# Instance normalisation: statistics of the last tile in one pass

## The chip, the core and the metric

The kernel runs on one core of one Trainium2 chip. The metric is device time in microseconds. Executions of one program spread here by about 2 us, with now and then one that is 4 to 12 us longer, so a time is quoted as a median with its range, and the difference of two kernels comes from runs taken in turn on the same chip. All runs count as fast. Times read off a trace count from the start of the profiled span; the metric is 1.7 us longer than that span.

## The reference

```python
x = np.random.randn(8, 64, 32, 64, 64).astype(np.float32)     # 512 instances of 131072 elements
mean = np.mean(x, axis=(2, 3, 4), keepdims=True)
var = np.var(x, axis=(2, 3, 4), keepdims=True)
out = ((x - mean) / np.sqrt(var + eps)).astype(np.float32)
```

268 MB are read and 268 MB are written. Little is computed per byte.

## The kernel before

Each tile is 128 partitions x 12288 elements (6 MB), three chunks of 4096 to a partition. 42 such tiles go through four buffers; two small parts of 2 MB go first. A tile is loaded whole, worked on, and stored. An instance lies over several partitions, so its sums are put together by a matmul with a matrix of averages (`avg`) and a small mask (`belongs`). Two such hand-overs follow each other: means, then the sums of squares around them. VectorE and ScalarE share the elements.

```python
    def tile_on_vector(eng, t, lane, c1, c3, c4, c16):
        # sums of chunk 0 and of a piece of chunk 2
        for j, part in ((0, chunk[0]), (3, t[:, COLS - TURN :])):
            eng.reduce_sum(out=column(a, SUMS, j), in_=part, axis=AXIS)._wait_ge(
                landed[lane], c16).then_inc(summed[lane], 1)
        over_instance(...)                                   # mask, matmul, sum, mask, sum: means
        eng.tensor_scalar(out=chunk[0], in0=chunk[0], scalar1=column(a, MEANS, 0), ...)   # centre
        eng.tensor_tensor_reduce(out=unused[2][:], in0=chunk[0], in1=chunk[0], ...)       # squares
        over_instance(...)                                   # the same again: variances
        eng.reciprocal(...); eng.tensor_mul(...)             # scale, shift
        eng.tensor_scalar(out=chunk[0], ...).then_inc(done[lane], 1)    # x * scale
        eng.tensor_scalar(out=chunk[1], ...).then_inc(done[lane], 1)    # x * scale + shift

    def tile_on_scalar(eng, t, lane, c1, c3, c4, c16, dst, last=False):
        # ... sums of chunk 1 and most of chunk 2; later squares of chunks 1 and 2; the root ...
        at = 0
        if last:
            at = CHUNK
            eng.dma_start(out=dst[:, :at], in_=chunk[0])._wait_ge(
                done[lane], c3 - 2).then_inc(stored[lane], 16)          # a third goes out early
        eng.activation(out=chunk[2], in_=chunk[2], func=Act.Identity, ...)   # x * scale + shift
        eng.dma_start(out=dst[:, at:], in_=t[:, at:])._wait_ge(done[lane], c3).then_inc(
            stored[lane], 16)
```

(The loads are issued by SyncE, each when its buffer has been stored.)

## Time and profile before

| | kernel before |
|---|---|
| median of 3 runs (range) | 1247.86 us (1247.49 to 1249.13) |
| the profiled execution | 1249.99 us, span 1248.3 us |
| DMA rate over the span | 430 GB/s |
| last tile in its buffer, work starts | 1211.60 |
| first store of the last tile issued | 1231.17 |
| last packet of the last store ends | 1246.84 |

A load or a store is cut into packets, which 16 DMA engines move. In the packet records of these traces a full tile is 128 packets of 48 KB, eight to an engine, and one small packet closes each engine's share. The *landing* of a tile is the moment when the last engine has closed its share of the load.

The prediction below shows the page's main lines, the last chain and the windows of the tail. What the statistics cost can be read from the groups of instructions with shapes kept apart (before the bar: line, engine, operation, shapes, count; after it: busy us in all and mean ns of one; then the idle time ahead of it).

```profile
L160 DVE TENSOR_REDUCE small<-slot 128x1 f32<-128x4096 f32 x42 | 185.6, 4420 | 288.7 <-DMA slot<-in_x_dram 288.7
L174 DVE CUSTOM_DVE_ANT_0 unused<-slot 128x4096 uint8<-128x4096 f32 x42 | 185.9, 4426 | 1.4
L167 DVE TENSOR_SCALAR slot<-slot,small 128x4096 f32<-128x4096 f32 x42 | 98.8, 2353 | 1.5
```

To take VectorE's statistics of one chunk the kernel reads it three times: 4.42 us for the sum, 2.35 us to centre it, 4.43 us for the squares.

### The profile page before, as it was taken

How to read it: one execution, taken by the hardware profiler on the slowest of the kernel's cores; microseconds unless marked ns; L12 is line 12 of the kernel's file. 1: busy time of each engine (PE TensorE's matmuls, PEld its weight loads, DVE VectorE, ACT ScalarE, POOL GpSimd, SP SyncE). 2: the span in 40 equal slices, each digit the busy share in tenths (PEclk: the TensorE clock that was granted, in tenths of full speed). 3: DMA queues.
4: the chain of work that ended last, by engine and by line, in shares of the span. 5: the costliest groups of instructions: out<-in, count | busy, mean ns of one | idle time of the engine just before them, and what ended most of it. 6: DMA issues, size and time to landing. Idle time of an engine off the chain costs nothing.

```text
span 1248.3 us, 1975 instructions
## 1 busy us (share of the span) xinstructions
PE 53.5 (4%) x180; PEld 44.9 (4%) x180; DVE 817.8 (66%) x734; ACT 754.8 (60%) x437; POOL 2.7 (0%) x15
## 2 busy tenths in 40 slices
PE   1000000000000000000000000000000000000000
PEld 0000000000000000000000000000000000000000
DVE  4886666666666666666666666666666666666664
ACT  4776655555665666666555566666665665556663
POOL 0000000000000000000000000000000000000000
DMA  9999999999999999999999999999999999999997
GB/s 400 423 429 449 432 428 428 432 443 433 430 428 443 435 430 428 435 441 432 428 432 438 438 430 428 430 447 430 430 430 436 439 432 430 428 446 432 430 432 340
DMA packets 13106, 536.89 MB, mean 430 GB/s; under 512 B 1456, under 2 KB 1456, under 8 KB 1712
## 3 DMA queue, kind: packets, MB, share of 16 engines
q1 hardware_dynamic: 6624, 268.44, 49.9%
q10 hardware_dynamic: 6480, 268.44, 49.7%
q14 instruction: 2, 0.02, 0.0%
HBM read 268.44 MB, written 268.44 MB: 430 GB/s over the span
## 4 chain that ended last, share of the span: by engine, by line
DMA 77%; DVE 11%; ACT 8%; PE 1%; issue 0%; SPq 0%; ACTq 0%
DMA slot<-in_x_dram 40%; DMA out_dram<-slot 38%; ACT unused L224 7%; DVE small L160 5%; DVE slot L196 2%; DVE slot L203 2%; PE psum L260 1%; ACT unused L217 0%; DVE small L140 0%; DVE small L128 0%; DVE small L134 0%; DVE small L146 0%; ACT slot L243 0%; ACT small L231 0%; DVE small L188 0%
## 5 line engine op out<-in xcount | busy, mean ns | idle before, releaser
L160 DVE TENSOR_REDUCE small<-slot 128x1 f32<-128x4096 f32 x84 | 255.3, 3081 | 288.7 <-DMA slot<-in_x_dram 288.7
L217 ACT ACTIVATE unused<-slot 128x4096 uint8<-128x4096 f32 x84 | 249.3, 2968 | 319.8 <-DMA slot<-in_x_dram 318.6
L224 ACT ACTIVATE unused<-slot,small 128x4096 uint8<-128x4096 f32 x84 | 310.8, 3701 | 65.3 <-DVE small L146 65.3
L174 DVE CUSTOM_DVE_ANT_0 unused<-slot 128x4096 uint8<-128x4096 f32 x42 | 185.9, 4426 | 1.4
L243 ACT ACTIVATE slot<-slot,small 128x4096 f32<-128x4096 f32 x42 | 159.7, 3802 | 21.1 <-DVE small L191 18.0
L203 DVE TENSOR_SCALAR slot<-slot,small 128x4096 f32<-128x4096 f32 x42 | 101.1, 2407 | 0.0
L167 DVE TENSOR_SCALAR slot<-slot,small 128x4096 f32<-128x4096 f32 x42 | 98.8, 2353 | 1.5
L260 PE MATMUL psum<-small,avg 128*128 128x12 f32 (+1 forms) x168 | 50.3, 375 | 1153.2 <-DVE small L128 1153.2
L196 DVE TENSOR_SCALAR slot<-slot,small 128x4096 f32<-128x4096 f32 x42 | 98.6, 2346 | 0.0
L260 PEld LDWEIGHTS psum<-small,avg 128*128 128x128 f32 x168 | 42.1, 311 | 1161.4 <-DVE small L128 1161.4
L134 DVE TENSOR_REDUCE small<-psum 128x3 f32<-128x12 f32 x84 | 14.2, 169 | 58.0 <-PE psum L260 58.0
L231 ACT ACTIVATE small<-small,eps_t 128x3 f32<-128x3 f32 x42 | 12.5, 299 | 62.6 <-DVE small L146 62.6
L128 DVE TENSOR_TENSOR small<-small,belongs 128x12 f32<-128x12 f32 x84 | 14.3, 170 | 31.4 <-ACT unused L224 29.5
L188 DVE RECIPROCAL small<-small 128x3 f32<-128x3 f32 x42 | 7.4, 175 | 15.4 <-ACT small L231 15.4
L140 DVE TENSOR_TENSOR small<-small,belongs 128x9 f32<-128x9 f32 x84 | 14.3, 170 | 2.9
L217 ACT ACTIVATION_READ_ACCUMULATOR unused<-slot 128x1 f32 x84 | 15.7, 187 | 0.0
L224 ACT ACTIVATION_READ_ACCUMULATOR unused<-slot,small 128x1 f32 x84 | 15.7, 187 | 0.0
L146 DVE TENSOR_REDUCE small<-small 128x3 f32<-128x9 f32 x84 | 13.6, 162 | 2.9
L280 DVE TENSOR_REDUCE small<-slot 128x1 f32<-128x1200 f32 (+1 forms) x4 | 4.7, 1208 | 7.6 <-DMA slot<-in_x_dram 7.6
L320 ACT ACTIVATE unused<-slot 128x1360 uint8<-128x1360 f32 (+1 forms) x4 | 4.2, 1059 | 5.8 <-DMA slot<-in_x_dram 5.3
L191 DVE TENSOR_TENSOR small<-small 128x3 f32<-128x3 f32 x42 | 6.8, 161 | 1.4
L326 ACT ACTIVATE unused<-slot,small 128x2608 uint8<-128x2608 f32 x2 | 4.9, 2469 | 1.9 <-DVE small L283 1.9
(32 smaller groups left out, 29.4 us busy)
## 6 DMA issues: line engine op xcount, KB each, us to landing
slot<-in_x_dram SPq DMA_DIRECT2D x42, 6144.0 KB, 47.1
out_dram<-slot ACTq DMA_DIRECT2D x41, 6144.0 KB, 47.1
out_dram<-slot ACTq DMA_DIRECT2D x3, 2048.0 KB, 23.7
out_dram<-slot ACTq DMA_DIRECT2D x1, 4096.0 KB, 11.8
slot<-in_x_dram SPq DMA_DIRECT2D x2, 1280.0 KB, 8.1
slot<-in_x_dram SPq DMA_DIRECT2D x2, 768.0 KB, 9.5
```

What stands on the lines that cost most here:

```text
L128: eng.tensor_tensor(out=block(a, by_both, n, m), in0=spread(a, at, m), in1=belongs[:, :, :m], op=Alu.mult,)._wait_ge(*wait).then_inc(steps ...
L134: eng.tensor_reduce(out=a[:, by_instance : by_instance + n], in_=p.rearrange("p (n m) -> p n m", m=m), axis=AXIS, op=Alu.add,)._wait_ge(st ...
L140: eng.tensor_tensor(out=block(a, by_chunk, n, n), in0=spread(a, by_instance, n), in1=belongs[:, :, :n].rearrange("p i c -> p c i"), op=Alu ...
L160: eng.reduce_sum(out=column(a, SUMS, j), in_=part, axis=AXIS)._wait_ge(landed[lane], c16).then_inc(summed[lane], 1)
L167: eng.tensor_scalar(out=chunk[0], in0=chunk[0], scalar1=column(a, MEANS, 0), scalar2=None, op0=Alu.add,)._wait_ge(centred[lane], c1).then_ ...
L174: eng.tensor_tensor_reduce(out=unused[2][:], in0=chunk[0], in1=chunk[0], scale=1.0, scalar=0.0, op0=Alu.mult, op1=Alu.add, accum_out=colum ...
L196: eng.tensor_scalar(out=chunk[0], in0=chunk[0], scalar1=column(a, SCALES, 0), scalar2=None, op0=Alu.mult,)._wait_ge(scaled[lane], c1).then ...
L203: eng.tensor_scalar(out=chunk[1], in0=chunk[1], scalar1=column(a, SCALES, 1), scalar2=column(a, SHIFTS, 1), op0=Alu.mult, op1=Alu.add,)._w ...
L217: eng.activation(out=unused[j - 1][:, : part.shape[1]], in_=part, func=Act.Identity, accum_out=column(a, SUMS, j),)._wait_ge(landed[lane], ...
L224: eng.activation(out=unused[j - 1][:], in_=chunk[j], func=Act.Square, bias=column(a, MEANS, j), accum_out=column(a, SQUARES, j),)._wait_ge ...
L243: eng.activation(out=chunk[2], in_=chunk[2], func=Act.Identity, scale=column(a, SCALES, 2), bias=column(a, SHIFTS, 2),)._wait_ge(shifted[l ...
L260: eng.matmul(out=p[:, col : col + THIRDS * m], lhsT=avg[PART][:], rhs=a[:, at + m : at + m + THIRDS * m], start=True, stop=True,)._wait_ge ...
```

## The change

For the last tile alone the statistics are taken in one pass. VectorE runs `bn_stats`, which gives mean and variance together, over chunk 0 and most of chunk 1. ScalarE finds the mean of its own pieces and then their squares around this own mean, without a hand-over between. The four pieces differ in size; masks weighted by size (`weighs`) put their means and variances together. All other tiles stay as they are; the setup on GpSimd gets six more small steps.

```diff
+    GROUP = 480
+    SHARE = 7 * GROUP
+    first_of = (0, CHUNK, 2 * CHUNK, CHUNK + SHARE)
+    sizes = (CHUNK, SHARE, CHUNK, CHUNK - SHARE)
+    groups = [(i * 512, 512) for i in range(CHUNK // 512)]
+    groups += [(CHUNK + i * GROUP, GROUP) for i in range(SHARE // GROUP)]
...
+    def last_on_vector(eng, t, lane, c1, c3, c4, c16):
+        for g, (at, size) in enumerate(groups):
+            i = eng.bn_stats(out=stats[:, g, :], in_=t[:, at : at + size])
...
+        step(eng.bn_aggr(out=a[:, 0:2], in_=stats[:, :split, :]))
+        step(eng.bn_aggr(out=a[:, 2:4], in_=stats[:, split:, :]))
+        eng.wait_ge(meant, 2)
+        weigh(means, BOTH)
+        hand_out(0, INST, CHUNKED, NEGATIVE, m, True)        # matmul: means of the instances
...                                                          # how far each piece's mean is off, squared
+        eng.wait_ge(spread_, 2)
+        step(eng.tensor_add(...))                            # its variance + that square
+        weigh(a[:, TOTAL : TOTAL + m], BOTH2)
+        hand_out(n * m, INST2, CHUNKED2, FOUND, n, False)    # matmul: variances
+        eng.wait_ge(took_root, 1)
...                                                          # reciprocal, shift, both chunks scaled
+    def last_on_scalar(eng, t, lane, c1, c3, c4, c16, dst):
...                                                          # own means, own squares, root, stores
-            on_tile(eng, slots[k % SLOTS][:], k % SLOTS, c, 3 * c, 4 * c, 16 * c, *more)
+            step = on_last if k == n_tiles - 1 else on_tile
+            step(eng, slots[k % SLOTS][:], k % SLOTS, c, 3 * c, 4 * c, 16 * c, *more)
```

More of the change, by code (lines that the diff above doesn't have):

```diff
@@ L72 @@
     belongs = sbuf("belongs", [P, THIRDS, THIRDS + 1])
+    GROUP = 480
+    SHARE = 7 * GROUP
+    first_of = (0, CHUNK, 2 * CHUNK, CHUNK + SHARE)
+    sizes = (CHUNK, SHARE, CHUNK, CHUNK - SHARE)
+    PIECES = len(sizes)
+    belongs4 = sbuf("belongs4", [P, THIRDS, PIECES])
+    weighs = sbuf("weighs", [P, THIRDS, PIECES])
+    groups = [(i * 512, 512) for i in range(CHUNK // 512)]
+    groups += [(CHUNK + i * GROUP, GROUP) for i in range(SHARE // GROUP)]
+    stats = sbuf("stats", [P, len(groups), 6])
+    late = sbuf("late", [P, 96])
     small = [sbuf(f"small{i}", [P, 72]) for i in range(LANES)]
@@ L98 @@
     moved = semaphores("moved", SLOTS)
+    went, meant, leaned, spread_, multiplied, took_root = semaphores("late", 6)
     shrunk = semaphores("shrunk")
@@ L210, in tile_on_vector, with tile_on_scalar @@
         )._wait_ge(shifted[lane], c1).then_inc(done[lane], 1)
-    def tile_on_scalar(eng, t, lane, c1, c3, c4, c16, dst, last=False):
+    def tile_on_scalar(eng, t, lane, c1, c3, c4, c16, dst):
         a = small[lane]
@@ L236, in tile_on_scalar @@
         )._wait_ge(gathered[lane], c1).then_inc(rooted[lane], 1)
-        at = 0
-        if last:
-            at = CHUNK
-            eng.dma_start(out=dst[:, :at], in_=chunk[0])._wait_ge(
-                done[lane], c3 - 2
-            ).then_inc(stored[lane], 16)
         eng.activation(
@@ L249, in tile_on_scalar @@
         )._wait_ge(shifted[lane], c1).then_inc(done[lane], 1)
-        eng.dma_start(out=dst[:, at:], in_=t[:, at:])._wait_ge(done[lane], c3).then_inc(
+        eng.dma_start(out=dst, in_=t)._wait_ge(done[lane], c3).then_inc(
             stored[lane], 16
@@ L266, in tile_on_tensor, with step, weigh, hand_out @@
             )._wait_ge(before[lane], c1).then_inc(after[lane], 1)
+    BIAS, BOTH, INST, CHUNKED, NEGATIVE, FAR, FAR2, TOTAL = 8, 10, 22, 25, 37, 41, 45, 49
+    BOTH2, INST2, CHUNKED2, FOUND, ROOTED, SCALED, SHIFTED = 53, 65, 68, 77, 80, 83, 86
+    def last_on_vector(eng, t, lane, c1, c3, c4, c16):
+        a, p = late, psum[lane]
+        n, m = THIRDS, PIECES
+        means, variances = a[:, 0 : 2 * m : 2], a[:, 1 : 2 * m : 2]
+        count = 0
+        def step(i):
+            nonlocal count
+            if count:
+                i._wait_ge(went, count)
+            i.then_inc(went, 1)
+            count += 1
+        def weigh(what, to):
+            step(
+                eng.tensor_tensor(
+                    out=block(a, to, n, m),
+                    in0=what.unsqueeze(1).to_broadcast([P, n, m]),
+                    in1=weighs[:],
+                    op=Alu.mult,
+                )
+            )
+        def hand_out(col, inst, at, to, k, negate):
+            eng.tensor_reduce(
+                out=a[:, inst : inst + n],
+                in_=p[:, col : col + n * m].rearrange("p (n m) -> p n m", m=m),
+                axis=AXIS,
+                op=Alu.add,
+            )._wait_ge(multiplied, 1 if col == 0 else 2).then_inc(went, 1)
+            nonlocal count
+            count += 1
+            step(
+                eng.tensor_tensor(
+                    out=block(a, at, k, n),
+                    in0=a[:, inst : inst + n].unsqueeze(1).to_broadcast([P, k, n]),
+                    in1=belongs4[:, :, :k].rearrange("p i c -> p c i"),
+                    op=Alu.mult,
+                )
+            )
+            step(
+                eng.tensor_reduce(
+                    out=a[:, to : to + k],
+                    in_=block(a, at, k, n),
+                    axis=AXIS,
+                    op=Alu.add,
+                    negate=negate,
+                )
+            )
+        for g, (at, size) in enumerate(groups):
+            i = eng.bn_stats(out=stats[:, g, :], in_=t[:, at : at + size])
+            if g == 0:
+                i._wait_ge(landed[lane], c16)
+        i.then_inc(went, 1)
+        count += 1
+        split = CHUNK // 512
+        step(eng.bn_aggr(out=a[:, 0:2], in_=stats[:, :split, :]))
[3 more added lines that the diff above has]
+        hand_out(0, INST, CHUNKED, NEGATIVE, m, True)
+        step(
+            eng.tensor_add(
+                out=a[:, FAR : FAR + m], in0=means, in1=a[:, NEGATIVE : NEGATIVE + m]
+            )
+        )
+        far = a[:, FAR : FAR + m]
+        step(eng.tensor_mul(out=a[:, FAR2 : FAR2 + m], in0=far, in1=far))
+        eng.wait_ge(spread_, 2)
+        step(
+            eng.tensor_add(
+                out=a[:, TOTAL : TOTAL + m], in0=variances, in1=a[:, FAR2 : FAR2 + m]
+            )
+        )
+        weigh(a[:, TOTAL : TOTAL + m], BOTH2)
+        hand_out(n * m, INST2, CHUNKED2, FOUND, n, False)
+        eng.wait_ge(took_root, 1)
+        step(
+            eng.reciprocal(out=a[:, SCALED : SCALED + n], in_=a[:, ROOTED : ROOTED + n])
+        )
+        step(
+            eng.tensor_mul(
+                out=a[:, SHIFTED : SHIFTED + n],
+                in0=a[:, NEGATIVE : NEGATIVE + n],
+                in1=a[:, SCALED : SCALED + n],
+            )
+        )
+        assert count == STEPS
+        for j in (0, 1):
+            part = t[:, j * CHUNK : (j + 1) * CHUNK]
+            eng.tensor_scalar(
+                out=part,
+                in0=part,
+                scalar1=column(a, SCALED, j),
+                scalar2=column(a, SHIFTED, j),
+                op0=Alu.mult,
+                op1=Alu.add,
+            )._wait_ge(went, STEPS).then_inc(done[lane], 1)
@@ new lines @@
+    WEIGHED, WEIGHED2, VARIED, STEPS = 4, 11, 14, 16
+    def last_on_scalar(eng, t, lane, c1, c3, c4, c16, dst):
+        a = late
+        mine = [(j, t[:, first_of[j] : first_of[j] + sizes[j]]) for j in (2, 3)]
+        for j, part in mine:
+            eng.activation(
+                out=unused[j - 2][:, : sizes[j]],
+                in_=part,
+                func=Act.Identity,
+                scale=1.0 / sizes[j],
+                accum_out=column(a, 0, 2 * j),
+            )._wait_ge(landed[lane], c16).then_inc(meant, 1)
+        for j, _ in mine:
+            eng.activation(
+                out=column(a, BIAS, j - 2),
+                in_=column(a, 0, 2 * j),
+                func=Act.Identity,
+                scale=-(sizes[j] ** -0.5),
+            )._wait_ge(meant, 2).then_inc(leaned, 1)
+        for j, part in mine:
+            eng.activation(
+                out=unused[j - 2][:, : sizes[j]],
+                in_=part,
+                func=Act.Square,
+                scale=sizes[j] ** -0.5,
+                bias=column(a, BIAS, j - 2),
+                accum_out=column(a, 0, 2 * j + 1),
+            )._wait_ge(leaned, 2).then_inc(spread_, 1)
+        eng.activation(
+            out=a[:, ROOTED : ROOTED + THIRDS],
+            in_=a[:, FOUND : FOUND + THIRDS],
+            func=Act.Sqrt,
+            bias=eps_t[:, 0:1],
+        )._wait_ge(went, VARIED).then_inc(took_root, 1)
+        eng.dma_start(out=dst[:, :CHUNK], in_=t[:, :CHUNK])._wait_ge(
+            done[lane], c3 - 2
+        ).then_inc(stored[lane], 16)
+        eng.activation(
+            out=t[:, 2 * CHUNK :],
+            in_=t[:, 2 * CHUNK :],
+            func=Act.Identity,
+            scale=column(a, SCALED, 2),
+            bias=column(a, SHIFTED, 2),
+        )._wait_ge(went, STEPS).then_inc(done[lane], 1)
+        eng.dma_start(out=dst[:, CHUNK:], in_=t[:, CHUNK:])._wait_ge(
+            done[lane], c3
+        ).then_inc(stored[lane], 16)
@@ L273, with last_on_tensor @@
+    def last_on_tensor(eng, t, lane, c1, c3, c4, c16):
+        for col, at, ready_at in ((0, BOTH, WEIGHED), (12, BOTH2, WEIGHED2)):
+            eng.matmul(
+                out=psum[lane][:, col : col + THIRDS * PIECES],
+                lhsT=avg[PART][:],
+                rhs=late[:, at : at + THIRDS * PIECES],
+                start=True,
+                stop=True,
+            )._wait_ge(went, ready_at).then_inc(multiplied, 1)
     HEAD = 2560
@@ L362, with over_tiles @@
     ]
-    def over_tiles(eng, on_part, on_tile, with_target=False):
+    def over_tiles(eng, on_part, on_tile, on_last, with_target=False):
         for m, (lane, t) in enumerate(parts):
@@ L381, in over_tiles @@
             c = k // SLOTS + 1
-            more = (out_t[k], k == n_tiles - 1) if with_target else ()
-            on_tile(eng, slots[k % SLOTS][:], k % SLOTS, c, 3 * c, 4 * c, 16 * c, *more)
+            more = (out_t[k],) if with_target else ()
+            step = on_last if k == n_tiles - 1 else on_tile
+            step(eng, slots[k % SLOTS][:], k % SLOTS, c, 3 * c, 4 * c, 16 * c, *more)
     def load_all(eng):
@@ L472, in set_up @@
         )
+        for to, c in ((slice(0, THIRDS), slice(0, THIRDS)), (slice(3, 4), slice(1, 2))):
+            step(eng.tensor_copy(out=belongs4[:, :, to], in_=belongs[:, :, c]))
+        for j, size in enumerate(sizes):
+            step(
+                eng.tensor_scalar(
+                    out=weighs[:, :, j : j + 1],
+                    in0=belongs4[:, :, j : j + 1],
+                    scalar1=float(size),
+                    scalar2=None,
+                    op0=Alu.mult,
+                )
+            )
         return count
@@ L477 @@
     nc.vector.wait_ge(ready, set_by)
-    over_tiles(nc.vector, part_on_vector, tile_on_vector)
+    over_tiles(nc.vector, part_on_vector, tile_on_vector, last_on_vector)
     nc.tensor.wait_ge(ready, set_by)
-    over_tiles(nc.tensor, part_on_tensor, tile_on_tensor)
+    over_tiles(nc.tensor, part_on_tensor, tile_on_tensor, last_on_tensor)
     nc.scalar.preload_act_table(Act.Sqrt)
     nc.scalar.wait_ge(ready, set_by)
-    over_tiles(nc.scalar, part_on_scalar, tile_on_scalar, with_target=True)
+    over_tiles(nc.scalar, part_on_scalar, tile_on_scalar, last_on_scalar, with_target=True)
     wait_for_stores(nc.scalar)
```

## The prediction

> **What bounds the kernel now.** I began with the page: busy time by engine, the slices and the DMA queues. They say that the stream of transfers is the limit.
>
> ```profile
> PE 53.5 (4%) x180; PEld 44.9 (4%) x180; DVE 817.8 (66%) x734; ACT 754.8 (60%) x437; POOL 2.7 (0%) x15
> DMA  9999999999999999999999999999999999999997
> q1 hardware_dynamic: 6624, 268.44, 49.9%
> q10 hardware_dynamic: 6480, 268.44, 49.7%
> ```
>
> VectorE works for 66% of the span, ScalarE for 60%, but the DMA row reads 9 in every slice but the last, and the two queues' packets fill 99.6% of sixteen engines' time. So only what lies outside this stream can be saved: its head, and the tail in the last slice (a 7). The change touches only the last of 42 full tiles, so I read the tail: first the chain that ended last, then the same stretch by windows.
>
> ```profile
> 1211.60 6.09 DVE small L160 x2
> ...
> 1219.19 7.50 ACT unused L224 x4
> ...
> 1228.87 2.27 DVE slot L196
> 1231.15 0.02 issue
> 1231.17 0.35 ACTq L240
> 1231.52 0.05 issue
> 1231.57 3.80 ACT slot L243
> ```
>
> The columns are start, length, what. The last tile is in the buffer at 1211.60. Sums take 6.09 us, squares 7.50 us, the two hand-overs through TensorE fill the places cut out, one third is scaled, and at 1231.17, 19.57 us after the landing, the first third's store is issued. The chain makes it look as if every microsecond saved there came off the end. The windows say whether DMA has something else to do meanwhile (columns: stretch and length, busy time and count of PE, PEld, DVE, ACT, POOL, clock, DMA share, GB/s):
>
> ```profile
> 1219.20:1226.70 7.50, 0.00 (x0) 0.00 (x0) 6.78 (x3) 7.48 (x4) 0.00 (x0) 1.00 1.00 433
> 1226.70:1231.20 4.50, 0.59 (x2) 0.50 (x2) 3.33 (x8) 0.30 (x1) 0.00 (x0) 1.00 0.15 66
> 1231.20:1232.00 0.80, 0.00 (x0) 0.00 (x0) 0.80 (x1) 0.43 (x1) 0.00 (x0) 1.00 0.00 0
> 1232.00:1237.00 5.00, 0.00 (x0) 0.00 (x0) 1.46 (x1) 3.37 (x1) 0.00 (x0) 1.00 1.08 459
> 1237.00:1246.90 9.90, 0.00 (x0) 0.00 (x0) 0.00 (x0) 0.00 (x0) 0.00 (x0) 1.00 0.94 404
> ```
>
> Until 1226.70 DMA is full (share 1.00) with the store of the tile before. Then come 4.50 us at a share of 0.15. That is not idle. The DMA view of 1227 to 1231.9 has what moves there:
>
> ```profile
> DMA packets 12, 0.29 MB, mean 60 GB/s; under 512 B 6, under 2 KB 6, under 8 KB 6
> ```
>
> Twelve packets start there: six of 48 KB and six small ones, which close an engine's share. Following the packet records, eleven or so of the 16 engines end their share of the store before between 1226.48 and 1227.31, but the last five end at 1228.35, 1229.55, 1230.21, 1231.15 and **1231.54**. A 48 KB packet takes 1.81 us on the late engines as on the others, and they have no gap between packets: they are simply behind. All tiles near the end show the same lag, 4 to 6 us between the first and the last engine. The last two stores then start on all engines at 1232.02 to 1232.17, 0.85 us after the issue, take 8 packets of 0.61 us and 8 of 1.22 us on each (14.67 us), and end at 1246.84. The span ends 1.45 us later.
>
> **What the Trainium skill says.** The page "DMA: Bandwidth & Descriptors", section "Why a DMA increments its semaphore by 16 and not by 1", says that a transfer runs on up to 16 engines that finish independently, each adding one to the semaphore behind its own data. The trace agrees: sixteen small packets close each store, here spread over 5 us. "VectorE: DVE Perf Modes", section "The perf-mode tier table", has tensor_reduce in the 1x mode only; here (4420 - 1743) / (4096 - 1536) = 1.046 ns per element, about one per cycle of the page's 0.96 GHz. "ScalarE: Activation LUTs", section "What ACT_TABLE_LOAD costs", gives 0.833 ns per element for an ACTIVATE; here (3617 - 2320) / 1536 = 0.844. No page that I found states the duration of bn_stats or bn_aggr, and no instruction of this trace is one, so I estimate both.
>
> **The change, part by part.** Times count from the landing at 1211.60.
>
> VectorE loses the two reductions (6.09), the centring of a third (2.35) and its squares (4.43 and the accumulator's read). It gains 15 bn_stats over 4096 + 3360 = 7456 elements. At the reduction's 1.046 ns that is 7.80 us. For the fixed cost, the second reduction of 1536 adds 6.08 - 4.42 = 1.66 us behind the first, 0.05 more than its elements; I choose 0.10 for an instruction that puts out six numbers, so 1.5 for 15. Statistics: **9.3 us**. Two bn_aggr over 48 and 42 numbers: a small instruction steps on in 0.20 (1218.58, 1218.79, 1218.99 in the timeline); I choose 0.37 each, 0.74 in all. Then come 13 small steps (weigh, sum, spread, sum, add, square, add, weigh, sum, spread, sum, reciprocal, shift) at 0.20: 2.6. TensorE is crossed twice; the weighing at 1217.71 to the reduction at 1218.58 is 0.87, less its own 0.20, so 0.67 each, 1.34 in all. The root adds 0.33 (1227.97 to 1228.50, less 0.20). Scaling and shifting the first third takes 2.41 (the row of L203, the same form). Sum: 9.3 + 0.74 + 2.6 + 1.34 + 0.33 + 2.43 = 16.74, so the first store is issued at about **1228.3**, 2.8 us earlier.
>
> ScalarE goes beside this: sums of 4096 and 736 elements (3.62 + 0.88, with an accumulator read), two one-element biases (0.55), squares of the same pieces (3.71 + 0.87 + 0.19). It ends at 9.9. VectorE wants its means after the aggregation at 10.0, its variances near 12. ScalarE should not be waited for, but with little in hand. It scales its third after the issue, as before: 0.40 + 3.80, so the second store is issued near 1232.6, while the first still runs.
>
> GpSimd gets six more small steps ahead of the loop, some 0.27 us each by its timeline, 1.6 in all: ready at 5.9 instead of 4.23, and the first piece lands at 7.10. Free. No other tile changes.
>
> What reaches the end? On the eleven early engines the last stores could start at 1228.3 + 0.85 = 1229.2 and end at 1243.9. The last engine is still busy until 1231.55. It takes the new packets without a gap and ends at 1231.55 + 14.67 = 1246.2. A store is done when all engines are. So of 2.8 us **only about 0.6 remains**: 1246.84 - 1246.2. From the median of 1247.86 that makes about 1247.2.
>
> **Rivals.** (a) All 2.8 us come off, to 1245.0: so it would be if the late engines had little lag in the timed runs, or caught up once the others were done. For it: the chain of waits, and I know the lag from one execution. Against it: the lag is there in each of the last tiles, and packets keep their 1.81 us when only few engines work. (b) bn_stats needs two cycles per element. Then statistics take 7.8 us more, the issue falls at 1236.1, the early engines decide too, and the time is about 4.9 us over the one before, 1252.8. Nothing in the profile speaks for it, but nothing rules it out. (c) ScalarE becomes the wait: it would have to be 2 us later than worked out to matter at all, and another 2.4 us of chain would be hidden behind the late engine anyway (issue up to 1230.7 still reaches it in time). (d) Nothing measurable: the three runs before lie 1.64 us apart, more than the gain.
>
> **Range and chances.** I give the late engine 65%, (a) or a part of it 25%, (b) under 10%. Together with run-to-run differences of about a microsecond: predicted 1247.0, a little below 1247.2 for the share of (a), range 1245.0 to 1248.6. Two per cent are 25 us, more than the whole tail from landing to last issue, so within 2% is almost sure: 0.98, with 0.01 on each side.
>
> **What would show it.** In the changed profile: bn_stats near 0.6 us each, 9.3 us together; ScalarE's squares done before VectorE adds its variances; the first store issued near 1228.3 on this trace's clock, or 16.7 us behind the landing; early engines closing the last store near 1243.9 and the last ones 2 us later; an end moved by well under the 2.8 us. The prediction is wrong if bn_stats takes over 0.75 us (the issue then comes after 1230.6), if the combining steps wait on ScalarE, or if the end moves by as much as the issue, which would mean that the late engines' lag isn't what holds the last store.

## The result and the profile after

| | before | changed |
|---|---|---|
| median of 6 runs each, in turn | 1247.69 us | 1247.62 us |
| range | 1247.19 to 1249.13 | 1247.16 to 1248.97 |
| profiled execution: time, span | 1249.99, 1248.3 | 1247.61, 1245.9 |
| work on the last tile starts | 1211.60 | 1208.34 |
| first store issued (after the start of work) | 1231.17 (19.57) | 1224.72 (16.38) |
| last packet ends (after the start of work) | 1246.84 (35.24) | 1244.31 (35.97) |

The ratio of the two kernels is 0.9999, with a 95% interval of 0.9986 to 1.0012: no difference. The 2.8 us of rival (a), 0.9978, lie outside it. (It is the mean time of one kernel's fast runs over that of the other's of the same rounds, so not quite the ratio of the medians.)

Beware of the spans. They differ by 2.4 us, near to what the chain saves, and tempt one to say that the chain's gain came off the end. But the execution profiled of the kernel before was one of its slower ones (1249.99 us where the median is 1247.69), and the last tile landed 3.26 us later in it. Nothing of the change happens before that landing, apart from setup. Counted from the start of the last tile's work, the end is no earlier in the changed kernel (35.97 us against 35.24).

The chain itself did what it was built for. Groups of the changed kernel:

```profile
L335 DVE BATCH_NORM_STATS2 stats<-slot 128x6 f32<-128x512 f32 x8 | 4.8, 678 | 7.2 <-DMA slot<-in_x_dram 7.2
L335 DVE BATCH_NORM_STATS2 stats<-slot 128x6 f32<-128x480 f32 x7 | 4.0, 642 | 0.0
L341 DVE BATCH_NORM_AGGREGATE late<-stats 128x2 f32<-128x48 f32 x1 | 0.4, 371 | 0.0
L342 DVE BATCH_NORM_AGGREGATE late<-stats 128x2 f32<-128x42 f32 x1 | 0.3, 344 | 0.0
```

The 15 `bn_stats` overlap a little: alone some 0.66 us, in a row 8.77 us. From its timeline (start, length, engine, line, operation), the moments that matter:

```profile
1208.34 8.76 DVE L335 BATCH_NORM_STATS2 stats<-slot 128x6 f32<-128x512 f32 x15 [7.20 <-DMA slot<-in_x_dram]
1217.71 0.19 ACT L408 ACTIVATION_READ_ACCUMULATOR unused<-slot,late 128x1 f32 x1
1219.79 0.17 DVE L355 TENSOR_TENSOR late<-late 128x4 f32<-128x4 f32 x1
1224.72 0.35 ACTq L422 DMA_DIRECT2D out_dram<-slot  x1
```

ScalarE's squares are complete at 1217.90, and VectorE adds variances only at 1219.79: ScalarE is not waited for. The chain view of the changed kernel ends so (start, length, what):

```profile
1208.34 8.77 DVE stats L335 x15
1222.28 2.42 DVE slot L375
1225.12 3.80 ACT slot L425
```

It follows instructions and stops at ScalarE's last one, 17 us before the end of the span. What happens after, the windows of the changed kernel tell (columns as in the prediction's windows; the DMA share and GB/s are the last two):

```profile
1224.70:1226.60 1.90, 0.00 (x0) 0.00 (x0) 1.90 (x1) 1.48 (x1) 0.00 (x0) 1.00 0.96 414
1226.60:1231.40 4.80, 0.00 (x0) 0.00 (x0) 0.41 (x1) 2.32 (x1) 0.00 (x0) 1.00 0.98 420
1231.40:1241.20 9.80, 0.00 (x0) 0.00 (x0) 0.00 (x0) 0.00 (x0) 0.00 (x0) 1.00 1.00 431
1241.20:1244.40 3.20, 0.00 (x0) 0.00 (x0) 0.00 (x0) 0.00 (x0) 0.00 (x0) 1.00 0.07 31
1244.40:1245.90 1.50, 0.00 (x0) 0.00 (x0) 0.00 (x0) 0.00 (x0) 0.00 (x0) 1.00 0.00 0
```

The stretch of little traffic that lay at 1226.70 to 1231.20 before (share 0.15) is full now (0.98). It has not gone: it has moved to the very end, 3.2 us at a share of 0.07. The DMA view has what starts in the changed kernel between 1241.7 and the end, and in the kernel before between 1246.6 and the end:

```profile
DMA packets 5, 0.07 MB, mean 16 GB/s; under 512 B 3, under 2 KB 3, under 8 KB 3
```

```profile
DMA packets 16, 0.00 MB, mean 0 GB/s; under 512 B 16, under 2 KB 16, under 8 KB 16
```

Each engine closes its share of a store with one small packet. Before, all sixteen are closed within 0.17 us, since all had waited for the same issue. Changed, thirteen engines are closed by 1241.7, and two 32 KB packets and three closing ones follow. One of the sixteen engines closes 1.9 us after all others, at 1244.31. It had also been the last with the store of the tile before, by 1.9 us.

### The profile page after: what moved, and what is told of

It is laid out like the page before. It is cut to its first block, busy times and chain, and to the rows that moved or that the text cites. A ratio compares the mean times of both kernels' runs of the same rounds, so it can differ in the third digit from the quotient of the medians.

```text
span 1245.9 us, 2001 instructions
## 1 busy us (share of the span) xinstructions
PE 53.5 (4%) x180; PEld 44.9 (4%) x180; DVE 815.1 (65%) x749; ACT 750.8 (60%) x439; POOL 4.0 (0%) x21
## 4 chain that ended last, share of the span: by engine, by line
another core or an unknown queue 46%; DMA 39%; DVE 7%; ACT 5%; SPq 1%; PE 1%; issue 1%; ACTq 0%; DVEq 0%
DMA slot<-in_x_dram 20%; DMA out_dram<-slot 19%; ACT unused L239 4%; DVE small L176 2%; DVE slot L219 1%; DVE slot L212 1%; DVE stats L335 1%; SPq L580 1%; PE psum L269 1%; ACT unused L232 0%; ACT slot L425 0%; DVE slot L375 0%; DVE small L156 0%; DVE small L144 0%
## 5 line engine op out<-in xcount | busy, mean ns | idle before, releaser
L176 DVE TENSOR_REDUCE small<-slot 128x1 f32<-128x4096 f32 x82 | 249.2, 3081 | 278.2 <-DMA slot<-in_x_dram 278.2
L232 ACT ACTIVATE unused<-slot 128x4096 uint8<-128x4096 f32 x82 | 243.3, 2968 | 308.6 <-DMA slot<-in_x_dram 307.4
L239 ACT ACTIVATE unused<-slot,small 128x4096 uint8<-128x4096 f32 x82 | 303.4, 3700 | 63.7 <-DVE small L162 63.7
L190 DVE CUSTOM_DVE_ANT_0 unused<-slot 128x4096 uint8<-128x4096 f32 x41 | 181.4, 4425 | 1.4
L252 ACT ACTIVATE slot<-slot,small 128x4096 f32<-128x4096 f32 x41 | 155.9, 3801 | 18.0 <-DVE small L207 18.0
L219 DVE TENSOR_SCALAR slot<-slot,small 128x4096 f32<-128x4096 f32 x41 | 98.7, 2407 | 0.0
L183 DVE TENSOR_SCALAR slot<-slot,small 128x4096 f32<-128x4096 f32 x41 | 96.5, 2353 | 1.5
L269 PE MATMUL psum<-small,avg 128*128 128x9 f32 (+1 forms) x164 | 49.1, 375 | 1122.0 <-DVE small L144 1122.0
L212 DVE TENSOR_SCALAR slot<-slot,small 128x4096 f32<-128x4096 f32 x41 | 96.2, 2346 | 0.0
L335 DVE BATCH_NORM_STATS2 stats<-slot 128x6 f32<-128x512 f32 (+1 forms) x15 | 8.8, 661 | 7.2 <-DMA slot<-in_x_dram 7.2
L393 ACT ACTIVATE unused<-slot 128x4096 uint8<-128x4096 f32 (+1 forms) x2 | 4.4, 2209 | 8.0 <-DMA slot<-in_x_dram 8.0
```

Of the source, the lines that this page charges most:

```text
L219: eng.tensor_scalar(out=chunk[1], in0=chunk[1], scalar1=column(a, SCALES, 1), scalar2=column(a, SHIFTS, 1), op0=Alu.mult, op1=Alu.add,)._w ...
L232: eng.activation(out=unused[j - 1][:, : part.shape[1]], in_=part, func=Act.Identity, accum_out=column(a, SUMS, j),)._wait_ge(landed[lane], ...
L239: eng.activation(out=unused[j - 1][:], in_=chunk[j], func=Act.Square, bias=column(a, MEANS, j), accum_out=column(a, SQUARES, j),)._wait_ge ...
L269: eng.matmul(out=p[:, col : col + THIRDS * m], lhsT=avg[PART][:], rhs=a[:, at + m : at + m + THIRDS * m], start=True, stop=True,)._wait_ge ...
L335: i = eng.bn_stats(out=stats[:, g, :], in_=t[:, at : at + size])
```

## The experiments

The theory (L): DMA is busy from start to end, each engine works off its own share, and the engine furthest behind sets the end. An earlier issue helps that engine only if it would otherwise run dry. The rival (C): the chain of the last tile sets the end, and each microsecond taken from it or added to it shows. In a trace the two can be told by three moments, taken from the packet records: the landing of the last tile, for which the work waits; the moment when the late engine is *free*, that is, done with the store of the tile before; and the end. 16 packets of the last stores take an engine 14.55 us without a pause. So *end - free - 14.55* is the hole in the late engine's work, what the chain can add to the end. (Where all engines start the last stores together, the 16 packets take 14.67 us. So 0.12 us of such a hole is slower packets and not a pause.) In the runs made after the first four (the small delays, the repeat of the changed kernel, the cut stream) theory L has numbers and is called L2: the late engine has 11 or 12 packets left after the landing, 19.9 to 21.8 us, and the chain shows only where the time from the landing to the first new packet is longer than that.

| profiled execution | landing | late engine free (after landing) | first store issued | end | hole |
|---|---|---|---|---|---|
| before | 1211.10 | 1231.54 (20.44) | 1231.17 | 1246.84 | 0.75 |
| before, again | 1210.57 | 1232.38 (21.81) | 1230.58 | 1246.93 | 0.00 |
| before + 2.2 us | 1207.76 | 1229.63 (21.87) | 1229.90 | 1245.57 | 1.39 |
| changed | 1207.84 | 1229.77 (21.93) | 1224.72 | 1244.31 | 0.00 |
| changed, again | 1207.73 | 1229.66 (21.93) | 1224.61 | 1244.20 | 0.00 |
| changed, few statistics | 1207.95 | 1229.85 (21.90) | 1216.99 | 1244.40 | 0.00 |
| changed + 2.2 us | 1208.20 | 1230.12 (21.92) | 1227.15 | 1244.68 | 0.01 |
| changed + 4.3 us | 1207.87 | 1229.78 (21.91) | 1228.94 | 1244.61 | 0.28 |
| changed + 8.8 us | 1209.88 | 1229.82 (19.94) | 1235.16 | 1250.82 | 6.45 |

The records do not number the engines, but packets can be linked by their times. In the first row the landing and the late engine so turn out to be two engines: the one that landed last, at 1211.10, was free at 1231.15 (11 packets), and the one that was free last, at 1231.54, had closed its load at 1209.78 (12 packets). The 20.44 us are a mixture of the two. In the next row both moments are on one engine.

### The kernel before, once more

No edit.

> The kernel before, unchanged, timed against itself and profiled once more. Theory L (the DMA engine that is furthest behind holds the end, and how far it is behind differs from one execution to the next): time within 0.05% of the kernel before, and in its profile the last engine closes the next-to-last store some 3 to 5 us after the first, not always the same amount. Theory C (the chain of waits of the last tile sets the end): the lag has no say, and the span should again be close to 1248.3 us.

Median 1249.34 us (1247.47 to 1250.21, 6 runs) against 1248.71 us (1247.41 to 1259.35, 11 runs) of the same kernel; ratio 0.9983 (0.9949 to 1.0018). Two kernels that are the same program differ in the median by 0.6 us here, so smaller differences than that cannot be told from times in such a job. Its windows:

```profile
1226.60:1231.40 4.80, 0.34 (x2) 0.24 (x2) 3.96 (x7) 0.72 (x2) 0.00 (x0) 1.00 0.19 82
1231.40:1232.40 1.00, 0.00 (x0) 0.00 (x0) 1.00 (x1) 1.00 (x1) 0.00 (x0) 1.00 1.15 492
```

As in the first profile most engines wait from 1226.6 on (the first and the last engine close the store of the tile before 5.9 us apart, more than the 3 to 5 us expected), but here the late engine is free only at 1232.38, 0.95 us after the other engines got their new packets, and runs on without a hole. In this execution the old chain was hidden altogether. The medians differ by the 0.05% that theory L allowed, with a noise larger than that. Rival C's expectation of the same span did come true (1248.5 against 1248.3 us), by another cause: both were executions with a lag of 5 to 6 us.

### Almost no statistics

The result is wrong on purpose (relative error 0.037).

```diff
         for g, (at, size) in enumerate(groups):
+            if g not in (0, CHUNK // 512):
+                continue
             i = eng.bn_stats(out=stats[:, g, :], in_=t[:, at : at + size])
...
-        mine = [(j, t[:, first_of[j] : first_of[j] + sizes[j]]) for j in (2, 3)]
+        mine = [(j, t[:, first_of[j] : first_of[j] + 256]) for j in (2, 3)]
```

(The aggregation and the outputs of ScalarE are cut to the same sizes.)

> The changed kernel with its last tile's statistics taken from a few hundred elements (wrong result on purpose): the chain from landing to the first store's issue gets some 7.5 us shorter, about 9 us instead of 16.4. Theory L: no time comes off, within 0.3 us of the changed kernel, because the stores then only queue behind the store before; the last engine ends as late as now. Theory C: about 7.5 us less, 1240 us.

Median 1247.66 us (1247.57 to 1248.41). The changed kernel had 1247.62 us in another job; the kernel before had 1248.71 us in this one, and the ratio to it, 0.9976 (0.9942 to 1.0010), is no difference either. Theory C's 1240 us lies far off. From the timeline:

```profile
1208.46 1.25 DVE L337 BATCH_NORM_STATS2 stats<-slot 128x6 f32<-128x512 f32 x2 [7.23 <-DMA slot<-in_x_dram]
1216.99 0.35 ACTq L424 DMA_DIRECT2D out_dram<-slot  x1
```

The first store was issued 8.5 us after the start of work, 7.9 us earlier than in the changed kernel, and nothing came off: its first packet moved only at 1226.58, when the first engine was done with the store of the tile before. The late engine ends 14.55 us after it is free, as before. This is the clearest verdict against rival C: even almost free statistics of the last tile are worth nothing here.

### Delay in the changed kernel: 2.2, 4.3 and 8.8 us

```diff
         split = CHUNK // 512
+        eng.reduce_sum(out=a[:, 90:91], in_=t[:, :2048], axis=AXIS)     # 2.2 us
```

(4096 in place of 2048 for 4.3 us; two of them, into two columns, for 8.8 us.)

> The changed kernel with one useless reduction over 2048 elements (2.2 us) in its chain: 17.8 + 2.2 = 20.0 us against 19.9 to 21.8 us of packets. Theory L2: no change against the changed kernel, within 0.3 us. Theory C: 2.2 us more.

> The changed kernel with a useless reduction over 4096 elements (4.3 us): 17.8 + 4.3 = 22.1 us against 19.9 to 21.8 us. Theory L2: 0.3 to 2.2 us over the changed kernel. Theory C: 4.3 us over it.

> The changed kernel with two useless reductions over 4096 elements (4.42 us each, 8.84 us) on VectorE between its statistics and their combination. Theory L: in the changed kernel's profile the last engine is free at 1229.77 and the first store issued at 1224.72, and a store needs 0.9 us from issue to its first packet; so the first 4.1 us of delay are hidden and some 4.6 us come through: about 1252.2 us. Theory C: all 8.8 us come through, 1256.4 us.

| | median (range) | over the changed kernel, medians |
|---|---|---|
| changed, same job as the two small delays | 1247.48 (1246.44 to 1248.22) | |
| + 2.2 us | 1247.89 (1247.29 to 1248.63) | 0.4 |
| + 4.3 us | 1247.79 (1247.67 to 1260.17) | 0.3 |
| + 8.8 us (another job; changed kernel 1247.6) | 1253.10 (1252.01 to 1253.98) | 5.5 |

In the profiles the issue moved back by 2.07, 4.19 and 8.52 us, counted from the start of work. The small delays cost next to nothing (0.4 us is a little over the 0.3 us expected of the first, but well within the runs' range), the large one some 5.5 of 8.8 us; against the kernel before in its own job, 1248.71 us, it cost 4.4 us. The knee is where theory L puts it. The delay of 4.3 us was expected to show 0.3 to 2.2 us and showed the least of that; its profile has a hole of 0.28 us, of which at most 0.16 us is a pause, because the late engine had 21.91 us of packets left after the landing. The 8.8 us came through somewhat more than the 4.6 us expected: in the execution profiled, the late engine had only 19.94 us left, and its pause before the last stores was 6.2 to 6.3 us. Two of the six runs with 4.3 us took 1258 and 1260 us; the kernel before has such runs as well (1257.82 and 1259.35 us in the first job). Windows with 4.3 us of delay:

```profile
1227.90:1229.80 1.90, 0.00 (x0) 0.00 (x0) 1.90 (x2) 0.46 (x1) 0.00 (x0) 1.00 0.08 34
1229.80:1244.50 14.70, 0.00 (x0) 0.00 (x0) 1.43 (x1) 3.34 (x1) 0.00 (x0) 1.00 1.00 427
```

The quiet stretch is back before the stores, and the stores then run as one block on all engines. The end is the same within 0.3 us. Whether the other engines are idle before the last stores or after them makes no difference.

### The changed kernel, once more

No edit.

> The changed kernel, unchanged, timed again. Theory L2 (after the last tile's landing the late engine still has 11 or 12 packets of the stores before, 19.9 to 21.8 us; the old chain with the start of a transfer takes 0.5 + 19.6 + 0.9 = 21.0 us, the new one 17.8 us, so both are hidden but for 0 to 1 us of the old): 0 to 1 us under the kernel before, 1247.6 us. Theory C (the chain sets the end): 3.2 us under it.

Median 1247.48 us (1246.44 to 1248.22, 5 runs) against 1247.78 us (1247.42 to 1249.95, 11 runs) of the kernel before; ratio 0.9994 (0.9981 to 1.0007). The middle of it is a gain of 0.7 us, yet no gain at all lies within the interval. Theory C's 3.2 us lie outside it.

### The same delay in the kernel before

```diff
+        if lane == 1 and isinstance(c1, int):                      # the last tile only
+            eng.reduce_sum(out=a[:, 70:71], in_=t[:, :2048], axis=AXIS)
         over_instance(
             eng, a, p[:, 0:12], SUMS, 4, MEANS, True, c1, (summed[lane], c4),
```

> The kernel before with the same useless reduction (2.2 us) in the chain of its last tile: 21.0 + 2.2 = 23.2 us against 19.9 to 21.8 us. Theory L2: 1.4 to 3.3 us come through over the point where the chain is just hidden, so some 1.4 to 2.2 us over the kernel before. Theory C: 2.2 us over it. A third view, that the tail has much slack in both kernels, says no change.

Median 1248.72 us (1248.62 to 1250.74) against 1247.78 us: 0.9 us, or 1.2 us between the lowest of each. The ratio is 1.0011 (0.9998 to 1.0024). So the times alone exclude neither theory C's 2.2 us nor no change at all; the profile decides. That is less than I expected, because in this execution, as in most of those profiled, the late engine had 21.87 us of packets left, and not 19.9: the old chain was hidden with nearly a microsecond to spare, and only what went beyond came through. Its windows show the hole itself:

```profile
1229.60:1230.70 1.10, 0.00 (x0) 0.00 (x0) 1.10 (x2) 0.40 (x1) 0.00 (x0) 1.00 0.00 0
1230.70:1245.60 14.90, 0.00 (x0) 0.00 (x0) 1.49 (x1) 3.40 (x1) 0.00 (x0) 1.00 0.99 422
```

The late engine is free at 1229.63, and from then to 1230.75 no engine moves data. In this execution the chain holds the end, as it does in the first profile and with 8.8 us of delay.

### The stream cut short: is the saving real?

In both kernels the tile before the last stores only its first third, so that 4.2 MB less lie in the way of the last stores. Their outputs are wrong, which doesn't matter for the times.

```diff
-        eng.dma_start(out=dst[:, at:], in_=t[:, at:])._wait_ge(done[lane], c3).then_inc(
+        end = CHUNK if lane == 0 and isinstance(c1, int) else COLS
+        eng.dma_start(out=dst[:, at:end], in_=t[:, at:end])._wait_ge(done[lane], c3).then_inc(
             stored[lane], 16
```

(The changed kernel has the same cut in its line for full tiles, `dst[:, :end]` and `t[:, :end]`.)

> The kernel before, but the last tile but one stores only a third of itself (wrong result on purpose): the stream behind the last landing gets 9.6 us shorter, 10.3 to 12.2 us, far under the chain's 21.0 us, so the chain is laid bare. Theory L2: landing + 21.0 + 14.7 us of stores + 1.5 us, about 1246 to 1248 us on the clock of the timed runs, only some 0 to 1.5 us under the kernel before in spite of 4.2 MB less to store. Theory C: as the kernel before.

> The changed kernel with the same cut. Theory L2: the change's whole saving on the chain, 3.2 us, now shows against the kernel before with the same cut, about 1243.5 us. If the new statistics save nothing in the timed runs after all (theory D), the two kernels with the cut are alike.

The first pair gave 1247.34 us (1246.61 to 1248.34) for the kernel before and 1246.10 us (1243.60 to 1254.03) for the changed one, with too much spread in the second. So both ran again, on another chip:

> The kernel before with the short store of the last tile but one, again, because the first pair's times were spread over 2 to 10 us. Theory L2: from the start of the last tile's work to the end of the last packet 19.6 + 0.9 + 14.7 = 35.2 us in the profile; lowest time near 1246.6 us, median near 1247.

> The changed kernel with the same cut, again. Theory L2: 32.1 us from the start of the last tile's work to the end of the last packet, lowest time near 1243.6 us, 3 us under the other; the median lower by 1.5 to 3.5 us. Theory D (the saving isn't there in timed runs): lowest times and medians alike.

| with the short store | kernel before | changed kernel |
|---|---|---|
| first pair, median (lowest) | 1247.34 (1246.61) | 1246.10 (1243.60) |
| second pair, median (lowest) | 1248.02 (1246.86) | 1245.20 (1243.53) |
| second pair, profiles: landing | 1209.29 | 1209.28 |
| first store issued | 1229.22 | 1226.04 |
| last packet ends | 1244.88 | 1241.70 |

In the two profiles of the second pair the last tile landed at the same moment, so they can be laid on each other: the issue is 3.18 us earlier and the end is 3.18 us earlier. The lowest times differ by 3.0 and 3.3 us, the medians by 1.2 and 2.8 us, with runs spread over 2 to 10 us. In the profiles of the first pair the landings are 1.5 us apart, but from the landing to the end there are 35.65 and 32.55 us, 3.1 us less. Here the whole saving of the chain shows. Windows, kernel before with the cut, then the changed kernel with it:

```profile
1209.65:1219.60 9.95, 0.60 (x2) 0.50 (x2) 9.11 (x7) 8.39 (x5) 0.00 (x0) 1.00 0.71 305
1219.60:1229.20 9.60, 0.60 (x2) 0.50 (x2) 7.71 (x10) 5.43 (x5) 0.00 (x0) 1.00 0.00 0
```

```profile
1209.65:1219.60 9.95, 0.14 (x1) 0.14 (x1) 9.65 (x18) 9.50 (x10) 0.00 (x0) 1.00 0.71 305
1219.60:1226.00 6.40, 1.06 (x4) 0.86 (x4) 4.43 (x14) 0.30 (x1) 0.00 (x0) 1.00 0.00 0
```

DMA starts nothing for 9.6 us in the one and 6.4 us in the other: a hole on every engine, and the chain decides how long it is. Theory D, that the new statistics save nothing in practice, falls. The difference within the pairs does not tell L from C: with the chain laid bare both expect it. The kernel before with the cut also shows how much the chain matters once it is bare: it stores 4.2 MB less and is at most 0.5 us faster than the whole kernel before (medians 1247.34 against 1247.87, and 1248.02 against 1248.26).

### One engine spared

If one engine is always the late one, its last packets could go elsewhere.

```diff
-        eng.dma_start(out=dst[:, CHUNK:], in_=t[:, CHUNK:])._wait_ge(
-            done[lane], c3
-        ).then_inc(stored[lane], 16)
+        for lo, hi in ((0, 120), (120, 128)):
+            eng.dma_start(out=dst[lo:hi, CHUNK:], in_=t[lo:hi, CHUNK:])._wait_ge(
+                done[lane], c3
+            ).then_inc(stored[lane], 16)
```

(The wait for the stores at the end counts one store more.)

> The changed kernel with its very last store (128 rows) issued as two, of 120 and of 8 rows: the first should go to fifteen DMA engines, and the eight rows to eight engines, one packet each, so one engine is spared its 8 packets (9.7 us) and eight engines get one packet more (1.2 us). Theory L with the spared engine the late one: the end moves from the late engine (1244.3) to the next ones plus a packet, 1.5 us earlier. Theory L with another engine the late one: the same time or up to 1.2 us later. Theory C: no change, since the chain to the first issue is the same.

A miss for both theories: 1258.29 us (1255.96 to 1262.93), some 10 us slower (the kernel before had 1248.71 us in this job). The stores were split as meant: 23 small packets, 15 and 8, close them. Windows of this run:

```profile
1231.50:1241.80 10.30, 0.00 (x0) 0.00 (x0) 0.00 (x0) 0.00 (x0) 0.00 (x0) 1.00 1.00 242
1241.80:1255.00 13.20, 0.00 (x0) 0.00 (x0) 0.00 (x0) 0.00 (x0) 0.00 (x0) 1.00 0.60 124
```

The engines are busy (share 1.00), yet at 242 GB/s instead of the 431 of the changed kernel in its window of 1231.40 to 1241.20. The median 32 KB packet took 2.48 us where it takes 1.21 us; only 14 of 128 kept to the old time. Most of the others took 2.3 to 2.6 us, twice as long, while one engine went through its eight packets in 10.3 us. It looks as if the others shared, two by two, something that they do not share in a store of 128 rows; no run tested that. Why a store of 120 rows makes packets slower stays open, and so does whether the late engine is always the same one. No version came out of this that beats both kernels: what remains to be won at the end is the lag, and the chain can't reach it.

## Why the prediction was right or wrong

**That the last engine decides, and most of the chain's gain is lost:** right, and shown. With 7.9 us less chain nothing changes, with 8.8 us more some 5.5 us come through, and with a shorter stream the whole 3.2 us show.

**The chain's sum:** 16.74 us predicted, 16.38 measured. (The prediction reads 2.41 us for scaling and puts 2.43 into its sum. Its limit of 0.75 us per `bn_stats` would put the issue at 1230.3 and not after 1230.6: 15 times 0.13 us on 1228.3. Neither mattered.) Statistics took 8.77 us instead of 9.3 (the fixed part of a `bn_stats` in a row is nearer 0.07 than 0.10 us: 8.77 - 7.80 us over 15). The two aggregations took 0.37 and 0.34 us, where 0.37 had been assumed. The early engines were said to close the last store 2 us ahead of the late one; fourteen of the other fifteen did so 2.4 to 3.2 us ahead, one 1.9 us. The early engines were not idle until the issue plus 0.85 us, as supposed: the landing came 3.26 us sooner in this execution, so the store was issued before they were free, and they went straight from one store to the next.

**Setup and ScalarE:** right. GpSimd is ready at 5.99 instead of 4.23, before the first piece lands, and ScalarE is done 1.9 us ahead of need.

**The 0.6 us that "remains": the step that was mis-sized.** It was one execution's hole, 1231.55 to 1232.17, taken for the kernel's. By the formula that hole is 0.75 us; in the next execution profiled of the same kernel it is 0.00. The table shows why. An engine that is behind delays its last load as well as its stores. What counts is only how much is left after the landing: 21.8 to 21.9 us in seven of the nine profiles, which fits 12 packets of 1.81 us; 19.94 us in one, which fits 11; and 20.44 us in the first, on two engines. Against it stand 0.5 + 19.6 + 0.85 = 21.0 us from landing to the first new packet with the old chain. So in an execution of the first kind the old chain is already hidden, by nearly a microsecond, and in one of the others it shows by 0.6 to 1.1 us. How many of the timed runs were of either kind is not on record. Measured: 0.07 us between the medians of the first comparison, 0.30 us in the second, both within their intervals. What the timed runs show is thus rival (d), nothing measurable. The predicted 1247.0 is 0.6 us below the measured 1247.62, and inside the range; but with a range of 3.6 us, no gain at all would have been inside it too, so the number is no support for the 0.6 us.

**Rival (a) was put the wrong way round.** I said that all 2.8 us would come off if the lag were small in the timed runs. But a smaller lag moves the landing, and with it the whole chain, forward as much as it moves the end. The first profile of the changed kernel has the smaller lag (3.2 us against 5.1 us between the first and the last engine on the store before) and no gain at all.

**My own criterion misled.** "An end moved by well under the 2.8 us" was to be the sign; the ends of the two profiles differ by 2.53 us. Only counting from the landing, or a repeat of the kernel before, shows that this is the difference of two executions.

**Open:** where the lag comes from. It is not made in the tail alone. In the first profile of the kernel before, the first and the last engine close a load 0.8 us apart at 50 us, 5.1 at 219 and 6.4 at the last load; in that of the changed kernel 1.0, 2.2 and 3.0 us. The profiles of the kernel before have 78 and 80 packets of 48 KB that took over 1.85 us, among some 10,600; those of the changed kernel have 28 and 23, and the lag is larger in the first two. But the kernel before with its 2.2 us delay had 21, so this goes with the execution, and I cannot say that the kernel sets it.

## What to carry to other kernels

In this kernel, where DMA is busy to the end, work on the last tile was worth only the hole that it left on the engine that was furthest behind. Elsewhere, too, it is worth a look: compare the time from the last landing to the store's first packet with the transfer time that is still queued behind that landing. When two profiles are compared, count from the event that precedes the change, because the spans of two executions can differ by as much as the gain looked for. A quick test ahead of such a change is to skip the work, wrong result and all: if that brings nothing, no better algorithm for this work will.

## What the Trainium skill lacked or had wrong

- "VectorE: DVE Perf Modes" (and the other VectorE pages that I searched) has no duration for bn_stats and bn_aggr, which the trace calls BATCH_NORM_STATS2 and BATCH_NORM_AGGREGATE. Here 15 over 512 or 480 fp32 elements took 8.77 us in a row, 0.58 us each, 0.66 us alone; aggregating 48 and 42 numbers took 0.37 and 0.34 us.
- "DMA: Bandwidth & Descriptors" says that the engines of a transfer finish independently, but not that an engine's delay stays with it for the rest of a saturated stream. In the first profile the engines close a load 5.1 us apart at 219 us and still 6.4 us apart at the last one. In the profiles here the first and the last engine finish the store of the tile before the last 2.2 to 5.9 us apart, and with the stream whole and the chain hidden that lag holds the end of the kernel.
- The same page does not say that a store over 120 rows can be much slower per packet than one over 128: 2.48 us instead of 1.21 us for a 32 KB packet, 242 GB/s instead of 431 (one profile).
